# HGRN heads in pairs, emitted behind the RWKV stage

## The chip, the cores and the metric

The kernel is one program on one core of a Trainium2 chip. The metric is the device time of one execution in microseconds. Engines are named as in the profile: PE (TensorE), PEld (its weight loads), DVE (VectorE), ACT (ScalarE), POOL (GpSimd), SP (SyncE, which issues nearly all transfers).

## The reference

One layer for 512 tokens of width 1024, in float32: a norm, one wide projection, three mixers side by side (HGRN2, RWKV7, latent attention), a gated sum of their outputs, an output projection, a second norm and a gated feed-forward.

```python
h = rms_norm(x, mix_pre_g[l])
z = h @ w_cols
zq, zf, zi, zog, zrw, zcq, zckv, zkr, zgate, zvres = jnp.split(z, IN_SPLITS, axis=-1)
o_hg = hgrn2_mixer(zq, zf, zi, zog, lower_bounds[l], hgrn_onorm_g[l])
o_rw, v_first = rwkv7_mixer(zrw, ...)
o_mla = mla_mixer(zcq, zckv, zkr, cos, sin, ...)
merged = (g_hg * (o_hg @ w_branch[l, 0]) + g_rw * (o_rw @ w_branch[l, 1])
          + g_mla * (o_mla @ w_branch[l, 2]))
x = x + rms_norm(merged @ w_out[l], mix_post_g[l])
```

The change lies in the HGRN mixer. For each of eight heads of width 128 it runs a gated linear recurrence over the tokens:

```python
f = lower_bound + (1.0 - lower_bound) * jax.nn.sigmoid(zf32)
k = (1.0 - lower_bound) * jax.nn.sigmoid(-zf32)
...
o = jnp.einsum('bhts,bhsv->bhtv', scores, v) + jnp.einsum('bhtd,bhdv->bhtv', q * jnp.exp(b), state)
state = jnp.exp(b_last[:, :, 0, :, None]) * state + jnp.einsum('bhsd,bhsv->bhdv', kc * jnp.exp(b_last - b), v)
```

The result of each head is normalised and multiplied with `silu(zog)`.

## The kernel before

All activations stand feature by token, 128 features on the partitions and 512 tokens along the row. Large products are made three times over with operands split into a high and a low part (`mm3`, L137 to L139); a pair of 128-wide output columns runs through `stream`, which loads slabs of two 128-row blocks of weights, splits them on ACT (L205) and DVE (L132) and issues 12 matmuls of 128x512 for each slab into two `mmD` banks. These **dense matmuls** come from, in program order: `dense_z` (the projection, written to DRAM as `z`), `dense_gate` (the three gates, as `gth`), `branch(0)` on HGRN's output `ohg`, `branch(1)` on RWKV's output `orw`, and later `branch(2)` on the attention's output, `project` and `ffn`.

Beside them run three mixers, whose steps are small and depend on one another:

- RWKV (`rwkv`): for four groups of four heads a preparation (`rwkv_prep`, tiles `pr`), an inverse, a merge and a chain over eight chunks of 64 tokens (`rwkv_chain`, tiles `zus` and `yb`), with a normalisation at the end of a group.
- HGRN (`hgrn_head`, tiles `ph` in PSUM and names that begin with `h`): one head after another. It loads `f`, `q`, `v` and the output gate from `z`; makes `f` and `k`; takes a diagonal gram, then goes through the levels m = 1, 2, 4 ... 64. At each level it takes a gram of `k` and `q` (16 matmuls of 32x32 for levels 1 to 16, copied under a mask into `sd` by DVE, L804; 8 and 4 matmuls for levels 32 and 64, copied by ACT, L812), then multiplies one half of `q` (L817) and one half of `k` (L818) by the running gate `F`. Then come three transposes of `k`, the states (L834 to L838), the output `po` (L841, L843), squares and sums on ACT (L848), the power on POOL (L279), a scaling on ACT (L851), transposes, and the product with the gate (L855), which goes to `ohg`.
- The latent attention, MLA (`mla_low`, `mla_qv`, and eight times `mla_head`, tiles `pm`, `pmt`, `pmo`).

What sets the order: the code is written stage by stage, but each stage sits in a **lane**, a range of priorities (`lane`), and a scheduler merges the lanes at build time by its own estimate of when things are ready. HGRN's loads and first steps are in lane 6, its chain in lane 2, RWKV in lanes 5, 3 and 1, dense matmuls in lanes 7 and 0, MLA in lane 4. The merged order is then fixed for each engine: PE, DVE, ACT, POOL and SP each take their instructions in that order.

What can overlap is also set by memory. A pool that is opened gets free memory, or memory of pools that were closed ahead of it in program order, and then it waits for their last users. PSUM has eight banks: two `mmD` banks (`pD`), one each for `pC` and `pY` (RWKV's chain), two for `pR` (RWKV's preparation), two for `pH` (HGRN). `hgrn_open` is called ahead of `rwkv`, so HGRN has its own two banks and its own memory from the start, and its heads can run beside RWKV. MLA needs four banks and takes those of `pH` and `pR` when both are closed (`e4`, `e3` in `run`). All HGRN tiles but `hsg` are single, so a head's `k` or `q` is overwritten only when the head before it is through with it.

## Time and profile before

| what | value |
|---|---|
| median of 3 runs | 1433.51 us (1432.66 to 1435.68) |
| the profiled execution, its time and its span | 1434.43 us, 1432.6 us |
| instructions | 27571 |
| HGRN's tile `ph` on PE, first gram to last | 119.0 to 636.6 us |
| outputs of heads stored to `ohg`, first and last issue | 193.3 to 665.9 us |
| projection (`dense_z`), last copy | 568.4 us |
| gates (`dense_gate`), first and last | 583.7 to 813.0 us |
| RWKV's chain, last chunk's first product | 823.9 us |
| MLA's product with the values, first and last | 776.0 to 972.3 us |

How to read the profile's rows: a row of groups gives line, engine, operation, tile written and tiles read, shape, count, then busy time in us and the mean of one in ns, then the idle time of the engine just before such instructions and what ended it. A matmul of float32 operands is recorded twice, so a gram of 16 matmuls shows as x32. Matmuls overlap at their ends, so a matmul's duration is longer than the step from one to the next.

### The profile page before, as it was taken

How to read it: one execution, taken by the hardware profiler on the slowest of the kernel's cores; microseconds unless marked ns; L12 is line 12 of the kernel's file. 1: busy time of each engine (PE TensorE's matmuls, PEld its weight loads, DVE VectorE, ACT ScalarE, POOL GpSimd, SP SyncE). 2: the span in 40 equal slices, each digit the busy share in tenths (PEclk: the TensorE clock that was granted, in tenths of full speed). 3: DMA queues.
4: the chain of work that ended last, by engine and by line, in shares of the span. 5: the costliest groups of instructions: out<-in, count | busy, mean ns of one | idle time of the engine just before them, and what ended most of it. 6: DMA issues, size and time to landing. Idle time of an engine off the chain costs nothing.

```text
span 1432.6 us, 27571 instructions
## 1 busy us (share of the span) xinstructions
PE 1394.2 (97%) x9672; PEld 1113.5 (78%) x9672; DVE 877.6 (61%) x1918; ACT 639.3 (45%) x1283; POOL 155.8 (11%) x1028
## 2 busy tenths in 40 slices
PE   7999989999999999999999999999999999999997
PEld 6777767777777776777877788887788888888886
DVE  5667977868688587774745657665475444443234
ACT  5563555553736346434543445443354333332222
POOL 2110111121212021111201010001010000000000
PEclk9999999999999999999999999999999999999999
DMA  6555462444543535345523445445544333334223
GB/s 189 153 170 155 125 186 84 146 141 121 168 140 113 153 116 168 94 139 171 166 75 102 135 160 194 152 124 178 197 148 133 96 98 99 98 96 155 96 96 110
DMA packets 172602, 194.93 MB, mean 136 GB/s; under 512 B 33072, under 2 KB 125744, under 8 KB 172464
## 3 DMA queue, kind: packets, MB, share of 16 engines
q1 hardware_dynamic: 171072, 190.02, 43.8%
q10 hardware_dynamic: 1392, 3.15, 0.7%
q8 instruction: 77, 1.26, 0.4%
q14 instruction: 61, 0.50, 0.1%
HBM read 151.30 MB, written 41.81 MB: 135 GB/s over the span
## 4 chain that ended last, share of the span: by engine, by line
PE 84%; DMA 7%; ACT 3%; DVE 2%; issue 2%; SPq 1%; POOL 0%; DVEq 0%; POOLq 0%; ACTq 0%
PE mmD L137 18%; PE mmD L139 18%; PE mmD L138 17%; PE po L137 4%; PE po L139 4%; PE po L138 4%; PE pr L194 2%; DMA zr<-z 1%; PE pmo L1090 1%; PE yb L704 1%; PE pm L139 1%; PE pm L137 1%; PE pm L138 1%; DMA z<-zst 1%; DMA hz<-z 1%
## 5 line engine op out<-in xcount | busy, mean ns | idle before, releaser
L137 PE MATMUL mmD<-xH,whD 128*128 128x512 f32 (+1 forms) x1232 | 486.5, 396 | 10.0 <-ACT whD L205 4.8
L138 PE MATMUL mmD<-xL,whD 128*128 128x512 f32 (+1 forms) x1232 | 474.4, 386 | 0.0
L139 PE MATMUL mmD<-xH,wlD 128*128 128x512 f32 (+1 forms) x1232 | 456.7, 389 | 2.0 <-DVE wlD L132 1.9
L132 DVE TENSOR_TENSOR wlD<-wsD,whD 128x512 fp32r<-128x512 f32 x384 | 263.6, 687 | 307.7 <-ACT whD L205 293.5
L205 ACT CAST whD<-wsD 128x512 fp32r<-128x512 f32 x384 | 237.6, 619 | 417.6 <-PE mmD L138 258.7
L137 PEld LDWEIGHTS mmD<-xH,whD 128*128 128x128 f32 x1232 | 232.1, 189 | 60.0 <-issue 6.2
L139 PEld LDWEIGHTS mmD<-xH,wlD 128*128 128x128 f32 x1232 | 230.8, 189 | 51.6 <-DVE wlD L132 4.6
L138 PEld LDWEIGHTS mmD<-xL,whD 128*128 128x128 f32 x1232 | 232.8, 189 | 41.0 <-issue 0.4
L149 POOL MEMSET token<- 1x1 f32 x912 | 82.4, 90 | 763.4 <-PE mmD L139 746.2
L139 PE MATMUL po<-whD,fL 128*128 128x512 f32 x176 | 68.3, 390 | 0.0
L138 PE MATMUL po<-wlD,fH 128*128 128x512 f32 x176 | 68.3, 390 | 0.0
L137 PE MATMUL po<-whD,fH 128*128 128x512 f32 x176 | 50.9, 391 | 0.2
L279 POOL TENSOR_TENSOR rrs<-rtm,mhalf 128x1 f32<-128x1 f32 x8 | 4.7, 591 | 405.4 <-DVE rtm L274 368.3
L237 ACT COPY zst<-mmD 128x512 f32<-128x512 f32 x64 | 37.3, 583 | 23.1 <-PE mmD L139 22.6
L628 DVE TENSOR_TENSOR invtmp<-inv 64x30 f32<-64x30 f32 (+14 forms) x120 | 38.5, 321 | 10.6 <-DMA inv<-Ld 8.5
L629 DVE TENSOR_TENSOR inv<-inv,invtmp 64x30 f32<-64x30 f32 (+14 forms) x120 | 38.6, 322 | 2.3
L137 PEld LDWEIGHTS po<-whD,fH 128*128 128x128 f32 x176 | 32.9, 188 | 8.0 <-DVE y L1185 0.6
L139 PEld LDWEIGHTS po<-whD,fL 128*128 128x128 f32 x176 | 33.0, 188 | 7.1
L138 PEld LDWEIGHTS po<-wlD,fH 128*128 128x128 f32 x176 | 33.0, 188 | 7.0
L702 DVE SCALAR_TENSOR_TENSOR PV<-zus,gC,St 64x64 f32<-64x64 f32 x96 | 27.1, 282 | 15.8 <-PE zus L696 13.7
L682 POOL TENSOR_TENSOR St<-PV,gC 64x128 f32<-64x128 f32 x48 | 23.4, 486 | 41.8 <-DVE PV L702 30.9
L793 PEld LDWEIGHTS ph<-hq,hk 128*32 128x32 f32 x1536 | 17.9, 111 | 12.7 <-issue 4.0
(343 smaller groups left out, 2023.7 us busy)
## 6 DMA issues: line engine op xcount, KB each, us to landing
wsD<-in_w_in_dram SPq DMA_DIRECT2D x176, 256.0 KB, 3.0
wsD<-in_w_ffn_in_dram SPq DMA_DIRECT2D x96, 256.0 KB, 2.8
z<-zst SPq DMA_DIRECT2D x63, 256.0 KB, 2.8
wsD<-in_w_branch_dram SPq DMA_DIRECT2D x48, 256.0 KB, 2.7
wsD<-in_w_ffn_out_dram SPq DMA_DIRECT2D x44, 256.0 KB, 2.6
zr<-z SPq DMA_DIRECT2D x26, 256.0 KB, 3.0
gth<-zst SPq DMA_DIRECT2D x24, 256.0 KB, 2.2
th<-gth SPq DMA_DIRECT2D x24, 256.0 KB, 3.4
```

What stands on the lines that cost most here:

```text
L132: (eng or self.nc.vector).tensor_tensor(dst, src, high.bitcast(F32), op=ALU.subtract)
L137: first = mm(ps, lhsT=lh, rhs=rh, start=start, stop=False)
L138: mm(ps, lhsT=lh, rhs=rl, start=False, stop=False)
L139: return first, mm(ps, lhsT=ll, rhs=rh, start=False, stop=stop)
L149: token = self.nc.gpsimd.memset(self.token, 0.0).ins
L194: last = c()
L205: nc.scalar.copy(h, st)
L237: self.nc.scalar.copy(st[:m], ps)
L628: V.tensor_tensor(tv, cv, rv, op=ALU.mult)
L629: V.tensor_tensor(U[:, :j, j + 1:], U[:, :j, j + 1:], tv, op=ALU.add)
L682: nc.gpsimd.tensor_tensor(St[H[e]], PV[e][H[e], :, c, :], gC[H[e], :, c + 1:c + 2].to_broadcast([64, 2, C]), op=ALU.mult)
L702: V.scalar_tensor_tensor(nxt, zus[H[e], 2, q, :], gc, St[H[e], q, :], op0=ALU.mult, op1=ALU.add)
```

## The change

Two heads go through each step together, as one tile that is twice as wide: `hgrn_head(h)` becomes `hgrn_heads(h0)`, called four times. Element-wise steps are done once for both heads, except where a per-feature constant differs (L766 and L768, now once for each head); the masked copies, the multiplies of a level and the running gate have twice the width. Matmuls and transposes are as many as before, and those with 512 output columns keep a bank for each head. `pH` has four banks in place of two. And `hgrn_open` is called behind `rwkv()` and behind the closing of `e3`, so HGRN's banks and memory are those that RWKV's preparation (`pR`, `rt`) has left. Transfers are as many and as large as before.

```diff
-        self.pH = es.enter_context(tc.tile_pool(name="pH", bufs=2, space=PSUM))
-        self.hsc = self.t(self.hg, [P, NT, P], "hsc")
+        self.pH = es.enter_context(tc.tile_pool(name="pH", bufs=4, space=PSUM))
+        self.hsc = self.t(self.hg, [P, HH, NT, P], "hsc")
...
-        f = self.h_load(1, h, "hf")
-        k = self.t(hg, [P, S], "hk")
+        f = self.h_load(1, h0, "hf")
+        k = self.t(hg, [P, HH, S], "hk")
         A.activation(k, f, AF.Sigmoid, scale=-1.0)
         A.activation(f, f, AF.Sigmoid)
-        V.tensor_scalar(f, f, oml, lb, op0=ALU.mult, op1=ALU.add)
+        for j in range(HH):
+            lb, oml = self.lb[:, h0 + j:h0 + j + 1], self.oml[:, h0 + j:h0 + j + 1]
+            V.tensor_scalar(f[:, j], f[:, j], oml, lb, op0=ALU.mult, op1=ALU.add)
+            V.tensor_scalar(k[:, j], k[:, j], oml, None, op0=ALU.mult)
...
+        q, k, f = flat(q), flat(k), flat(f)
+        N = HH * S
         def gram():
-            g = self.t(pH, [P, NT, HB], "ph")
-            for o in range(0, S, HB):
+            g = self.t(pH, [P, W, HB], "ph")
+            for o in range(0, N, HB):
...
-                g = self.t(pH, [P, NT, m], "ph")
-                for i in range(NT):
+                g = self.t(pH, [P, W, m], "ph")
+                for i in range(W):
...
+        for j, po in enumerate(pos):
+            for i in range(NT):
+                A.activation(on[:, j, i, :], po[:, i, :], AF.Copy, scale=rs[:, j * NT + i:j * NT + i + 1])
...
         self.rwkv_open(e1, e2, e3)
+        self.rwkv()
+        e3.close()
         self.hgrn_open(e4)
-        self.rwkv()
-        for h in range(8):
-            self.hgrn_head(h)
+        for h in range(0, 8, HH):
+            self.hgrn_heads(h)
         e4.close()
-        e3.close()
```

The order on PE before, at the diagonal gram of the last head (`ph` written from `hq` and `hk`; `zus` is RWKV's chain, `mmD` a dense matmul):

```order
L793 MATMUL ph_9326<-hq_9309,hk_9303 32x32 x6
L691 MATMUL zus_7191<-zsb_7198,LM_5909 64x64 x4
L793 MATMUL ph_9326<-hq_9309,hk_9303 32x32 x10
L137 MATMUL mmD_3676<-xH_7_108,whD_3679 128x512
L138 MATMUL mmD_3676<-xL_15_116,whD_3679 128x512
L139 MATMUL mmD_3676<-xH_7_108,wlD_3680 128x512
L137 MATMUL mmD_3676<-xH_8_109,whD_3679 128x512
```

Fifteen dense matmuls and eight of RWKV's follow before this head's next gram. The order on PE now, at the third pair, from the end of the second one's output to the third one's last level (`yb` is written here from `y`, in RWKV's last normalisation):

```order
L873 MATMUL ph_8476<-cst,hkT_8434 128x128 x3
L782 MATMUL ph_8507<-cst,hz_8497 128x128 x4
L803 MATMUL ph_8520<-hq_8494,hk_8486 32x32 x32
L803 MATMUL ph_8555<-hq_8494,hk_8486 32x32 x32
L803 MATMUL ph_8593<-hq_8494,hk_8486 32x32 x32
L726 MATMUL yb_7681<-cst,y_7420 128x128 x4
L803 MATMUL ph_8631<-hq_8494,hk_8486 32x32 x32
L726 MATMUL yb_7696<-cst,y_7420 128x128 x4
L803 MATMUL ph_8669<-hq_8494,hk_8486 32x32 x32
L803 MATMUL ph_8707<-hq_8494,hk_8486 32x32 x32
L820 MATMUL ph_8745<-hq_8494,hk_8486 32x32 x16
L820 MATMUL ph_8768<-hq_8494,hk_8486 64x64 x8
```

Between the steps stands no dense matmul any more. The first pair's first step on PE comes behind the last matmul of RWKV's preparation and behind RWKV's last merge; the last dense matmul of the gates comes ahead of the second pair's gram of level 16; and the next dense matmul, the first of branch 0, behind the fourth pair's last transpose.

A second place, MLA's last heads. On PE before (`pm` scores, `pmt` transposes, `pmo` products with the values), around a block's transpose in the seventh head:

```order
L1074 MATMUL pm_11721<-krL_10572,qr_10606 128x384
L1086 MATMUL pmt_11694<-cst,mp_11690 128x128
L1070 MATMUL pm_11745<-uh_2071_11674,uh_2065_11657 128x512
L1071 MATMUL pm_11745<-ul_2072_11675,uh_2065_11657 128x512
L1072 MATMUL pm_11745<-uh_2071_11674,ul_2066_11658 128x512
L1073 MATMUL pm_11745<-krH_10571,qr_10606 128x512
L1074 MATMUL pm_11745<-krL_10572,qr_10606 128x512
L139 MATMUL mmD_10230<-xH_1654_9980,wlD_10301 128x512
L137 MATMUL mmD_10230<-xH_1655_9981,whD_10300 128x512
```

Ten dense matmuls (the fence shows the first two) stand there before the block's product `pmo`. On PE now, the same place in the seventh head:

```order
L1092 MATMUL pm_11461<-krL_10288,qr_10322 128x512
L139 MATMUL mmD_11633<-oL_1720_10562,whD_11681 128x512
L140 MATMUL mmD_11633<-oH_1712_10554,wlD_11682 128x512
L139 MATMUL mmD_11634<-oL_1720_10562,whD_11681 128x512
L140 MATMUL mmD_11634<-oH_1712_10554,wlD_11682 128x512
L1108 MATMUL pmo_11394<-mpT_11412,mv_10455 128x128
L1104 MATMUL pmt_11430<-cst,mp_11426 128x128 x2
L138 MATMUL pm_11495<-cqH_10196,whU_1983_11491 128x512
```

Only four stand there, and two more in the rest of that head; they belong to branch 2 (`oH`, `oL`), since those of branches 0 and 1 are used up. From one head's first score to the next one's, the dense matmuls were 40, 46, 148, 54, 56, 55 and 48, and are 60, 54, 57, 18, 6, 6 and 6. From the output projection on, the order is that of before.

## Prediction

> **What bounds the kernel now.** I read the page first, then the stages by window, then single groups by shape.

> ```profile
> PE 1394.2 (97%) x9672; PEld 1113.5 (78%) x9672; DVE 877.6 (61%) x1918; ACT 639.3 (45%) x1283; POOL 155.8 (11%) x1028
> PE 84%; DMA 7%; ACT 3%; DVE 2%; issue 2%; SPq 1%; POOL 0%; DVEq 0%; POOLq 0%; ACTq 0%
> 120.00:660.00 540.00, 526.93 (x5206) 401.65 (x5205) 408.34 (x1003) 270.68 (x580) 88.33 (x539) 0.99 0.46 135
> 660.00:980.00 320.00, 319.27 (x1860) 260.52 (x1859) 195.81 (x459) 150.97 (x310) 36.09 (x275) 1.00 0.47 144
> 1160.00:1200.00 40.00, 40.00 (x178) 33.12 (x177) 17.93 (x27) 13.64 (x23) 0.00 (x0) 1.00 0.34 98
> L793 PE MATMUL ph<-hq,hk x1536: 196/196/218, 119.0 to 636.6; 128*32 128x32 f32 x192
> 110.00:670.00 560.00, 73.00 (x1976) 56.81 (x1976) 27.68 (x80) 33.95 (x136) 0.99 0.47 137
> ```

> TensorE is the bound: 97% busy, 84% of the chain that ended last. In the windows (after the length: PE, PEld, DVE, ACT, POOL busy, clock, DMA share, GB/s) it idles 13.1 us of 540 while HGRN runs and 0.7 us of the 320 of MLA. So a change pays only if PE does less, or idles less; there is 13 us of idleness to win in HGRN's stretch, and none after it. A dense matmul takes 40.00/178 = 0.225 us.

> The HGRN grams run from 119.0 to 636.6 us, eight heads in some 550 us. The last window is that of the HGRN tile `ph` alone: 73.0 us of PE. A head is a long chain of short steps over PE, DVE, ACT and POOL, and it costs nothing now because dense matmuls (`mmD`) stand between its steps. The kernel is fast because the chains have **cover**; the question for the change is who covers them in the new order.

> **The change part by part.** *The arithmetic* stays: as many matmuls of the same sizes, so PE's own work is unchanged. *The order* is what moves. PE takes its instructions in program order; the rows shown with the change say that up to the end of RWKV's preparation no HGRN step is left on PE, that pairs 1 and 2 stand among dense matmuls, and that behind the last gate matmul, before the first matmul of branch 0, stand the end of pair 2 (from its gram of level 16), all of pair 3 and all of pair 4, with no dense matmul among them. What is queued behind them is MLA's first matmul and branch 0, which itself needs all of `ohg`.

> So I price **a pair that runs alone**, from these rows (durations of one head's steps):

> ```profile
> L798 DVE TENSOR_TENSOR hq<-hq,hf 128x512 f32<-128x512 f32 x8 | 5.6, 701 | 0.0
> L817 DVE TENSOR_TENSOR hq<-hq,hF 128x256 f32<-128x256 f32 x48 | 20.2, 421 | 4.2 <-PE ph L810 4.1
> L804 DVE COPY_PREDICATED hsd<-hgm,ph 128x128 f32<-128x128 uint8 x40 | 11.8, 294 | 5.1 <-PE ph L793 4.9
> L838 DVE SCALAR_TENSOR_TENSOR hst<-hst,hF,ph 128x128 f32<-128x128 f32 x16 | 5.4, 340 | 0.1
> L855 DVE SCALAR_TENSOR_TENSOR hsg<-ph,hon,hsg 128x512 f32<-128x512 f32 x8 | 6.0, 744 | 1.1 <-PE ph L854 0.9
> L831 ACT COPY hkT<-ph 128x384 f32<-128x384 f32 x8 | 3.8, 480 | 6.9 <-PE ph L829 6.8
> L848 ACT ACTIVATE hkT<-ph 128x128 f32<-128x128 f32 x32 | 8.4, 277 | 6.1 <-PE ph L843 6.0
> L848 ACT ACTIVATION_READ_ACCUMULATOR hkT<-ph 128x1 f32 x32 | 6.6, 207 | 0.0
> L851 ACT ACTIVATE hkT<-ph,hrs 128x128 f32<-128x128 f32 x32 | 9.3, 372 | 6.8 <-POOL token L149 6.8
> L279 POOL TENSOR_TENSOR rs<-ss,mhalf 128x8 f32<-128x8 f32 x8 | 13.2, 1652 | 19.9 <-DVE ss L538 18.7 <-PE mmD L138 1.2
> 615.71 0.46 PE L793 MATMUL ph<-hq,hk 128*32 128x32 f32 x32
> 616.10 0.50 PE L137 MATMUL mmD<-xH,whD 128*128 128x512 f32 x1
> ```

> - DVE: a level's two multiplies become 512 wide, 0.70 us as in L798; 7 levels x 2 = 9.8. The full product of `q` and `f` is 1024 wide: 0.70 + 2 x (0.70 - 0.42) = 1.26. Five masked copies, 256 wide, about 0.43 each (0.29 and half of what 256 more elements cost): 2.2. Diagonal 0.4, states 2 x (0.28 + 2 x 0.34) = 1.9, last output 0.74. Together 16.3 us.
> - PE: a head's gram of 16 matmuls (32 records) is 0.46 us long and lets the next start after 0.39, so a pair's is 0.85; six are 5.1, the two block levels about 1.0, and transposes, `dS`, `po` about 2.4 as far as nobody overlaps them. 8.5 us.
> - ACT: two `hkT` copies 0.96, eight squares 8 x (0.277 + 0.207) = 3.9, eight scalings 3.0. 7.8 us.
> - POOL: the power on 128x8, 1.65 us.

> Each waits for the one before: a level's multiplies need the last gram read, the next gram needs both products. In series 34.3 us; the second head's states and squares lie partly beside the first head's, hand-overs add; I take **33 us**. Bounds: 27 (DVE plus its waits for grams, the tail halved) and 43 (two heads in sequence, 20 us each by the same rows at half width, and some waits).

> The uncovered stretch is then: rest of pair 2, from its last gram, 19 (two levels more, then the tail); pairs 3 and 4, 66; RWKV's last three chunks and its normalisation, in line with them on DVE and PE, 4; hand-over to MLA, 9:

> ```profile
> 668.36 4.38 DMA mz<-z
> 676.40 0.79 PE pm L953 x8
> ```

> MLA's pools take HGRN's memory and its four PSUM banks, so its first load starts when HGRN has ended, and its first matmul came 8 us after the load's start; before, dense matmuls covered that. In sum **98 us**. In it lies PE work that was paid before too: 56% of the grams and 102 larger steps, about 4.6 heads of 73.0/8 = 9.1 us, x 0.39/0.46 since records overlap: 36, and RWKV's rest, 5. Loss: 98 - 41 = **57 us**.

> **The clock** is the second term. The one place where PE had much the same sparse work is 208 to 214:

> ```profile
> 208.00:210.00 2.00, 0.88 (x5) 0.32 (x3) 1.22 (x3) 0.00 (x0) 0.18 (x2) 1.00 0.58 146
> 210.00:212.00 2.00, 0.75 (x50) 0.64 (x52) 1.94 (x7) 0.90 (x2) 0.00 (x0) 1.00 0.87 268
> 212.00:214.00 2.00, 1.48 (x59) 1.35 (x52) 1.97 (x3) 2.00 (x5) 0.00 (x0) 0.67 0.77 251
> 214.00:216.00 2.00, 2.00 (x9) 1.90 (x9) 2.00 (x6) 1.97 (x3) 0.00 (x0) 0.50 0.57 214
> 218.00:220.00 2.00, 2.00 (x7) 1.61 (x6) 0.00 (x1) 1.32 (x3) 0.09 (x1) 0.62 0.11 37
> 210.98 0.46 PE L793 MATMUL ph<-hq,hk 128*32 128x32 f32 x32 [1.20 <-DVE hk L818]
> 213.49 1.87 PE L535 MATMUL pr<-cst,t 128*128 128x2 f32 x8 [0.52 <-ACT t L531]
> 100.41 1.05 PE pr L535 x8
> ```

> After 4 us at 40% busy the granted clock fell to 0.50, and eight small matmuls took 1.87 us instead of 1.05. A lone pair keeps PE busy a quarter to a third of the time, so I expect half clock through most of the stretch: 2.4 pairs x 8.5 us of PE on the path x 0.78 = **16 us**, between 0 and 20. [...]

> **MLA** is the third. 384 dense matmuls of branches 0 and 1 are left to cover eight heads; the order spends most of them early: from the fourth head on it leaves 18, and then 6 to each of the last four, where a head has 57 now:

> ```profile
> 888.67:911.51 22.84, 14.18 (x57) 10.37 (x56) 1.36 (x2) 0.00 (x0) 1.00 0.51 163
> 888.67:911.51 22.84, 22.84 (x124) 19.54 (x123) 14.20 (x34) 9.93 (x22) 1.76 (x19) 1.00 0.51 163
> ```

> (the first row is `mmD` alone, the second all). A head's own PE work is 22.84 - 57 x 0.225 = 10.0, with 6 dense ones 11.4; its own DVE and ACT work some 9 and 7. The floor is 11.4, full series 27; two score banks let blocks overlap, so near the floor: 14. The fourth head, 10.0 + 18 x 0.225 = 14, loses nothing then; four heads x 2.6 = 10, and the last head's transposes and copies, which have nothing behind them, 3: **13 us** (0 to 4 x 15.6 + 3 = 65).

> **What may come back**: with HGRN gone, some of the 13.1 us of idleness before 660 us, and switches between dense and small work; I take 4 (0 to 15). PE, not DVE's instruction count, was the bound there, so the halved count of DVE and ACT steps is worth nothing by itself. More SP and ACT work is not issued: loads stay 128x512 each, two per name.

> Sum: 57 + 16 + 13 - 4 = 82 us, on the profiled execution's 1434.4 (its span of 1432.6 and 1.8 around it; the median of the runs is 0.9 lower): **1517 us**.

> **The rivals.**
> - *The clock stays full* in the stretch: the sum without that term, 1501. [...] Against: the fall at 213 us.
> - *The pair does not do what it says*: its two heads run after one another, since a step twice as wide costs DVE nearly twice as much (421 against 701 ns). 40 us for 33, x 2.6: 1535; with MLA heads at 20 us, five x 6 more, 1565. For it: the single banks of transposes and outputs in MLA. Against: the fixed part of each step, about 140 ns, is saved.
> - *A short stretch*: engines overlap better, 27 us a pair, full clock, MLA at its floor: 57 - 2.6 x 6 = 41, less 4: 1470.
> - *Faster*: HGRN's departure gives back all 13.1 us of idleness up to 660 us, and the 2 us that dense matmuls lost at half clock at 215: 1419. It decides if the stretch loses under 15 us, so if it lasts 56 and a pair some 16 us: DVE's own 16.3, with PE, ACT and POOL wholly beside it. The chain's waits speak against it.

> **How the numbers follow.** Forecast 50%, full clock 22%, pair in sequence or slow MLA 17%, short stretch 6%, faster 3%, no change 2%. The range takes in the bounds of chain, clock and MLA as far as they are not all at one end: 1470 to 1585. Faster by over 0.2% (about what a measurement can tell from no change) 0.03, within 0.02, slower 0.95.

> **What would show it.** Right: past 650 us a stretch of some 100 us or more in which PE is mostly idle, released by DVE and ACT, tile names `ph`, clock near 0.5; MLA heads at 13 to 15 us with PE idle a few us each; everything from the output projection on as before. Wrong: PE over 80% busy there (then the chain is shorter than the rows say), clock 1.00 (first rival), or MLA heads at 20 us. The forecast fails as a whole if dense matmuls are not exhausted where the order says.

## The result, and the profile after

| | kernel before | kernel after |
|---|---|---|
| median of the runs | 1434.6 us (1432.66 to 1438.4, 4 runs) | 1506.96 us (1503.12 to 1509.23, 4 runs) |
| profiled execution: span, mean granted clock | 1432.6 us, 0.996 | 1501.3 us, 0.967 |

The change makes the kernel slower: ratio 1.0498, with a 95% interval of 1.0465 to 1.0531. The forecast was 1517 us. The profiled execution took 1503.12 us, the shortest of the four.

The page after (busy time and share by engine, two rows of the span in 40 slices, the chain by engine):

```profile
PE 1411.8 (94%) x9672; PEld 1130.6 (75%) x9672; DVE 873.1 (58%) x1794; ACT 622.6 (41%) x1231; POOL 154.0 (10%) x1024
PE   7999999999999999999555999998999999999998
PEclk9999999999999999999665899999999999999999
PE 80%; DMA 5%; DVE 5%; issue 5%; ACT 3%; POOL 1%; SPq 1%; DVEq 0%; POOLq 0%; ACTq 0%
```

PE has as many instructions as before and is busy 17.6 us longer (1411.8 against 1394.2): the same work in longer records. Most of it is the lower clock: in the stretch below PE is busy 38.8 us at a clock of 0.50, where a pair's gram takes 1.08 us, against 0.76 at full clock, which makes some 11 us (an estimate from these three numbers). It also idles 51.1 us longer (89.5 against 38.4); the two make up the 68.7 us by which the span grew. Three slices of the page, from 713 to 826 us, hold nearly all of it: PE half busy and the clock at 0.5 to 0.6.

The windows (length, then PE, PEld, DVE, ACT, POOL busy, clock, DMA share, GB/s): up to the last dense matmul of the gates; from there to MLA's first dense cover; MLA's last heads; and two short ones inside the stretch.

```profile
120.00:697.50 577.50, 572.55 (x4647) 433.60 (x4647) 394.38 (x859) 255.40 (x484) 96.67 (x646) 1.00 0.48 143
697.50:823.20 125.70, 68.31 (x1310) 58.49 (x1308) 67.71 (x150) 45.50 (x132) 10.11 (x11) 0.67 0.23 75
985.00:1042.50 57.50, 53.69 (x324) 46.31 (x323) 37.70 (x111) 30.65 (x76) 0.80 (x9) 1.00 0.09 28
740.00:760.00 20.00, 10.79 (x201) 9.94 (x202) 10.46 (x22) 7.06 (x14) 0.00 (x0) 0.50 0.22 66
780.00:800.00 20.00, 10.36 (x258) 9.43 (x259) 9.36 (x18) 3.87 (x9) 0.00 (x0) 0.50 0.01 2
```

Ahead of the stretch PE idles 4.95 us in 577.5, where the kernel before idled 13.1 in 540. In the stretch it idles 57.4. DVE, ACT and POOL are not full there either: each waits for another. The edges of the stretch are these two matmuls (PE's instructions in order of time):

```profile
697.68 0.39 PE L140 MATMUL mmD<-xH,wlD 128*128 128x512 f32 x1
...
819.36 3.54 PE L971 MATMUL pm<-ones,msq 128*128 128x1 f32 x16 [9.53 <-DMA mkv<-z]
```

From the end of the first to the start of the second pass 121.3 us. Where the time of a lone pair goes is seen on DVE in order of time: the diagonal grams (L807) of pairs 3 and 4, two levels of pair 4, and its end.

```profile
725.56 0.42 DVE L807 TENSOR_TENSOR hsd<-ph,cst 128x256 f32<-128x256 f32 x1
...
771.11 0.42 DVE L807 TENSOR_TENSOR hsd<-ph,cst 128x256 f32<-128x256 f32 x1 [0.80 <-PE ph L803]
...
775.38 1.22 DVE L788 SCALAR_TENSOR_TENSOR hsg<-hsg,hz 128x1024 f32<-128x1024 f32 x1 [2.72 <-ACT hsg L787]
...
779.43 0.44 DVE L814 COPY_PREDICATED hsd<-hgm,ph 128x256 f32<-128x256 uint8 x1 [1.29 <-PE ph L803]
779.77 0.68 DVE L827 TENSOR_TENSOR hq<-hq,hF 128x512 f32<-128x512 f32 x1
780.37 0.68 DVE L828 TENSOR_TENSOR hk<-hk,hF 128x512 f32<-128x512 f32 x1
782.34 0.44 DVE L814 COPY_PREDICATED hsd<-hgm,ph 128x256 f32<-128x256 uint8 x1 [1.29 <-PE ph L803]
...
808.84 0.75 DVE L874 SCALAR_TENSOR_TENSOR hsg<-ph,hon,hsg 128x512 f32<-128x512 f32 x1 [3.46 <-PE ph L873]
809.87 0.75 DVE L874 SCALAR_TENSOR_TENSOR hsg<-ph,hon,hsg 128x512 f32<-128x512 f32 x1 [0.28 <-PE ph L873]
```

A level takes 2.91 us, of which DVE works 1.6 and waits 1.29 for the next gram at a clock of 0.50. From one pair's diagonal gram to the next one's it is 45.6 us, and from the last one's to its last output 39.5 (770.31 and 810.62 are the ends of the third and the fourth pair).

Behind the stretch little is lost. MLA's last five heads (the last 100 of its 160 products) go through the window 985 to 1042.5 at 11.5 us each, with PE idle 0.8 us a head. MLA's last product was at 972.3 us before and is at 1042.6 now (matmuls that write `pmo`, of before and of after):

```profile
L1090 PE MATMUL pmo<-mpT,mv x160: 270/275/377, 776.0 to 972.3; 128*128 128x128 f32 x160
```

```profile
L1108 PE MATMUL pmo<-mpT,mv x160: 270/275/377, 921.5 to 1042.6; 128*128 128x128 f32 x160
```

That is 70.3 us later; the rest of the span is 460.3 us before and 458.7 after. So the whole loss stands ahead of MLA's end.

### The profile page after: what moved, and what is told of

The parts are those of the page before. It is cut to its first block, busy times and chain, and to the rows that moved or that the text cites. A ratio compares the mean times of both kernels' runs of the same rounds, so it can differ in the third digit from the quotient of the medians.

```text
span 1501.3 us, 27415 instructions
## 1 busy us (share of the span) xinstructions
PE 1411.8 (94%) x9672; PEld 1130.6 (75%) x9672; DVE 873.1 (58%) x1794; ACT 622.6 (41%) x1231; POOL 154.0 (10%) x1024
## 3 DMA queue, kind: packets, MB, share of 16 engines
q8 instruction: 77, 1.26, 0.4%
## 4 chain that ended last, share of the span: by engine, by line
PE 80%; DMA 5%; DVE 5%; issue 5%; ACT 3%; POOL 1%; SPq 1%; DVEq 0%; POOLq 0%; ACTq 0%
PE mmD L138 18%; PE mmD L140 17%; PE mmD L139 17%; PE po L138 4%; PE po L140 3%; PE po L139 3%; PE pr L195 2%; PE yb L705 1%; DMA zr<-z 1%; PE pm L138 1%; PE pm L139 1%; PE pm L140 1%; DMA z<-zst 1%; PE pmo L1108 1%; PE yb L690 1%
## 5 line engine op out<-in xcount | busy, mean ns | idle before, releaser
L138 PE MATMUL mmD<-xH,whD 128*128 128x512 f32 (+1 forms) x1232 | 488.8, 398 | 3.7 <-DVE rs L1206 1.2
L140 PE MATMUL mmD<-xH,wlD 128*128 128x512 f32 (+1 forms) x1232 | 449.9, 387 | 1.6 <-DVE wlD L133 1.5
L138 PEld LDWEIGHTS mmD<-xH,whD 128*128 128x128 f32 x1232 | 231.7, 189 | 56.5 <-POOL token L150 4.7
L140 PEld LDWEIGHTS mmD<-xH,wlD 128*128 128x128 f32 x1232 | 230.8, 188 | 51.1 <-DVE wlD L133 4.0
L139 PEld LDWEIGHTS mmD<-xL,whD 128*128 128x128 f32 x1232 | 232.6, 189 | 40.3 <-DVE xL L133 0.2
L140 PE MATMUL po<-whD,fL 128*128 128x512 f32 x176 | 68.3, 390 | 0.0
L139 PE MATMUL po<-wlD,fH 128*128 128x512 f32 x176 | 68.3, 390 | 0.0
L138 PE MATMUL po<-whD,fH 128*128 128x512 f32 x176 | 50.9, 391 | 0.2
L629 DVE TENSOR_TENSOR invtmp<-inv 64x30 f32<-64x30 f32 (+14 forms) x120 | 38.8, 323 | 13.4 <-DMA inv<-Ld 10.8
L803 PE MATMUL ph<-hq,hk 128*32 128x32 f32 x1536 | 23.3, 215 | 23.7 <-DVE hk L828 18.7
L630 DVE TENSOR_TENSOR inv<-inv,invtmp 64x30 f32<-64x30 f32 (+14 forms) x120 | 38.8, 323 | 2.7
L138 PEld LDWEIGHTS po<-whD,fH 128*128 128x128 f32 x176 | 32.9, 188 | 8.0 <-DVE y L1203 0.6
```

What stands on the lines that cost most here:

```text
L138: first = mm(ps, lhsT=lh, rhs=rh, start=start, stop=False)
L139: mm(ps, lhsT=lh, rhs=rl, start=False, stop=False)
L140: return first, mm(ps, lhsT=ll, rhs=rh, start=False, stop=stop)
L629: V.tensor_tensor(tv, cv, rv, op=ALU.mult)
L630: V.tensor_tensor(U[:, :j, j + 1:], U[:, :j, j + 1:], tv, op=ALU.add)
L803: mm(g[b:b + HB, o // P, :], lhsT=k[:, t], rhs=q[:, t], start=True, stop=True)
```

## The experiments

Each was run beside the kernel before on the same chip, and ratios are to that. The changed kernel was not run again with them: differences to it are to its 1506.96 us.

### The place alone: single heads behind RWKV

The changed kernel with `hgrn_head`, `h_load` and `hsc` of the kernel before; `pH` keeps four banks.

```diff
-    def hgrn_heads(self, h0):
+    def hgrn_head(self, h):
...
         self.rwkv()
         e3.close()
         self.hgrn_open(e4)
-        for h in range(0, 8, HH):
-            self.hgrn_heads(h)
+        for h in range(8):
+            self.hgrn_head(h)
```

> Heads one by one as before, but their pool opened behind the RWKV stage, with four banks, as in the change. The order on PE leaves about five and a half heads behind the last gate matmul without a dense matmul. Cover theory (the loss comes from the place, not from the width): a lone head takes about 24 us by the rows, so the uncovered stretch grows from 125 to some 150 us and the time is about 1530 us (1515 to 1545), slower than the change. Rival (the wide steps cost the time): the time returns towards that of before, 1460 us or less.

Measured: 1559.62 us, ratio 1.0862 (1.0826 to 1.0898), above the range that was expected. The rival falls: the place alone costs 123 us, and the width, which was thought to be what costs, gives 53 us back. Lone heads follow one another on DVE like this (diagonal grams of the last three heads, and two levels of the last one):

```profile
796.78 0.29 DVE L797 TENSOR_TENSOR hsd<-ph,cst 128x128 f32<-128x128 f32 x1 [3.74 <-PE ph L793]
...
822.68 0.29 DVE L797 TENSOR_TENSOR hsd<-ph,cst 128x128 f32<-128x128 f32 x1 [3.09 <-PE ph L793]
...
848.12 0.29 DVE L797 TENSOR_TENSOR hsd<-ph,cst 128x128 f32<-128x128 f32 x1 [3.51 <-PE ph L793]
...
856.44 0.30 DVE L804 COPY_PREDICATED hsd<-hgm,ph 128x128 f32<-128x128 uint8 x1 [0.86 <-PE ph L793]
...
858.26 0.30 DVE L804 COPY_PREDICATED hsd<-hgm,ph 128x128 f32<-128x128 uint8 x1 [0.86 <-PE ph L793]
```

A lone head takes 26 us, two 52, and a lone pair 40 to 46; a level of one head takes 1.82 us and of a pair 2.91. A head's ends and waits weigh more than the prediction's bound for two heads in sequence, 20 us each, allowed.

Pairs at the old place, beside RWKV, were not run (their pool holds 44 KB for each partition, the sum of its tiles, and would lie beside RWKV's pools), so what they would be worth there stays open.

### More dense work behind the gates

Behind `dense_gate`, eight groups of 24 dense matmuls of the same shape, paced as they are; nothing reads their result.

```diff
+    def idle_work(self, groups):
+        for g in range(groups):
+            p = self.t(self.pD, [P, S], "mmD")
+            for k in range(KD):
+                xh = self.h[0][k]
+                group = self.mm3(p, xh[:, :P], xh[:, P:2 * P], xh, xh, k == 0, k == KD - 1)
...
             self.dense_gate(n)
+        self.idle_work(8)
```

> The change, with 192 more dense matmuls behind the gates whose result nobody reads (43 us of PE work at 0.225 us each). Cover and clock theory: they fill the idle time at the third pair, the granted clock stays at 1.00 there, a level's step falls from 2.9 us to about 2.3, and the time is within 10 us of the change's 1507 although PE has 43 us more to do; the fourth pair stays bare, with the clock near 0.5. Rival (PE work adds up, the clock does nothing): about 1550 us.

Measured: 1530.49 us, ratio 1.0656 (1.0623 to 1.0688): neither. 43 us of work cost 23.5. The windows show it lying beside the ends of pairs 2 and 3, where PE is now full at full clock, while pair 4 is as bare as before:

```profile
720.00:740.00 20.00, 20.00 (x144) 15.72 (x142) 8.47 (x27) 6.83 (x28) 3.36 (x18) 1.00 0.09 28
740.00:760.00 20.00, 20.00 (x280) 16.01 (x279) 12.49 (x18) 5.25 (x8) 4.71 (x22) 1.00 0.37 114
800.00:820.00 20.00, 7.34 (x304) 6.66 (x304) 10.72 (x19) 3.23 (x8) 0.00 (x0) 0.51 0.01 2
```

About half of the work fell into holes; the rest, since PE is full there, stood ahead of the pairs' steps in PE's queue. From diagonal gram to last output, pair 2 took 68.7 us in place of 53.0, pair 3 49.5 in place of 44.8, and pair 4 40.3 in place of 39.5. So this work, though it filled holes, made the chains longer by about half of itself; what matters is where it stands, as the runs on the clock below show.

### The same cover, later

Ten of the twelve gate streams are held until the first pair has begun.

```diff
+        for n in gates[:-HELD]:
+            self.dense_gate(n)
...
         for h in range(0, 8, HH):
             self.hgrn_heads(h)
+            if h == 0:
+                self.hold = self.mark
+                self.lane(7)
+                for n in gates[-HELD:]:
+                    self.dense_gate(n)
+                self.hold = None
```

> The change, with the last ten of twelve gate streams made to wait for the first step of the first pair, so that RWKV's stage cannot use them up. By the order, pairs 1 to 3 then have dense matmuls between their steps, the fourth has none, and a piece of RWKV's chain of some 25 us has few. Cover theory: 1470 us (1455 to 1485). Rival (the wide chain or the banks cost the time wherever it stands): no change, 1507 us.

Measured: 1518.03 us, ratio 1.0569 (1.0537 to 1.0601): 11 us slower than the change, where 37 faster were expected. The expectation failed. Two windows of it, the end of RWKV's preparation and pair 4:

```profile
560.00:580.00 20.00, 1.92 (x46) 1.63 (x48) 10.96 (x33) 0.00 (x0) 0.96 (x1) 0.50 0.22 46
...
780.00:800.00 20.00, 8.32 (x336) 7.34 (x336) 9.90 (x16) 4.41 (x11) 0.00 (x0) 0.68 0.16 54
```

RWKV's preparation, with its inverse and last merge, now stands bare, and though nothing dense is in its way, pair 1's diagonal gram comes only 10 us earlier (592.4 against 602.6). The hole moved; it did not close. That suggested another reading: not the supply of cover but the length of two chains, one behind the other, sets the time. The next two runs test it.

### No cover at all, in both orders

All twelve gate streams (130 us of PE) are held until the last HGRN output is made, once in the changed kernel and once in the kernel before.

```diff
-        for n in (*range(8, 16, 2), *range(0, 8, 2), *range(16, 24, 2)):
-            self.dense_gate(n)
...
             self.hgrn_heads(h)
+        self.hold = self.mark
+        self.lane(7)
+        for n in (*range(8, 16, 2), *range(0, 8, 2), *range(16, 24, 2)):
+            self.dense_gate(n)
+        self.hold = None
```

> The changed kernel with all 12 gate streams (576 dense matmuls, 130 us of PE) held until the last pair's last output. Theory: RWKV's preparation and then the four pairs are two chains in line, and their length, not the dense work, sets the time; the gates only lay beside them. RWKV's preparation should then end at some 590 us as before, bare from about 500 on, the pairs take 45 us each with little beside them, to about 770, and the gates follow at full speed to 900, with the hand-over to MLA hidden: 1575 us, 1555 to 1590. Rival: the chains are shorter when nothing dense stands between their steps (preparation over by 560, pairs 33 us each, 690), so the gates end about where MLA starts now: 1500 to 1510.

> The kernel before, with the same 12 gate streams held until the last single head's last output. Theory: there the heads run beside RWKV's preparation, so both chains are over by some 620 us, and the gates then lie beside RWKV's chunks and MLA, which have their own work: only 500 to 620 is thinner on PE, 15 to 40 us lost, 1450 to 1475 against 1436. Rival: what counts is only how much dense work is left as cover, not which chains run side by side; then this kernel loses as much against the one before as the changed kernel with its gates last loses against the changed one, 70 us: 1505.

Measured: the changed kernel with its gates last 1581.0 us (ratio 1.1015, 1.0983 to 1.1047), the kernel before with its gates last 1464.83 (1.021, 1.0175 to 1.0245). Both are where the theory put them, and both rivals fall (the second kernel is 2.1% slower, 1.75 to 2.45). The HGRN grams of the first and of the second (matmuls on `ph`: shortest, median and longest in ns, then the first and the last start):

```profile
L807 PE MATMUL ph<-hq,hk x1536: 189/241/263, 582.4 to 753.7; 128*32 128x32 f32 x192
```

```profile
L797 PE MATMUL ph<-hq,hk x1536: 189/196/262, 119.7 to 608.3; 128*32 128x32 f32 x192
```

With no gate beside it, RWKV's part ahead of the first pair (preparation, inverse and merge of its last group) still ends only at 582 us, 18 us earlier than in the change, and the four pairs then take until 776 us, 48 us a pair. The granted clock is 0.54 there from 500 to 582 us; how much of that length is the clock's was not measured. What the first pair waits for is the last group's inverse, a chain of 60 steps on DVE (from 537.8 to 564.7 us; 546.9 to 581.2 in the change), and its transfer out and back. PE has nothing to do meanwhile, for 22.10 us:

```profile
572.69 0.28 PE L193 MATMUL yb<-lsq,LM 32*32 32x32 f32 x2 [22.10 <-DVE lsq L653]
```

RWKV's last merge in the kernel before, in the change and here (the second time is the start of the last matmul):

```profile
L194 PE MATMUL yb<-LM,lsq x248: 191/191/212, 221.0 to 656.3; 32*32 32x32 f32 x124
```

```profile
L195 PE MATMUL yb<-LM,lsq x248: 191/191/212, 198.4 to 598.8; 32*32 32x32 f32 x124
```

```profile
L196 PE MATMUL yb<-LM,lsq x248: 191/191/257, 198.7 to 581.0; 32*32 32x32 f32 x124
```

So RWKV's part does end earlier in the change, where HGRN is not beside it, by 57 us, but the pairs that follow it need 211 us there. Behind the pairs of this run, 130 us of gates that earlier lay beside the chains are still to be done. In the old order the last of eight single heads takes its last gram at 608 us, because the heads ran beside RWKV's preparation all the time from 119.7 us on. So taking the gates away from the chains costs 30 us in the old order and 74 in the new.

### Two banks, and a second load buffer

Two edits of single sizes in the changed kernel: `pH` back to two banks; two buffers for `lnx`, whose loads DVE waits for in RWKV's last normalisation.

```diff
-        self.pH = es.enter_context(tc.tile_pool(name="pH", bufs=4, space=PSUM))
+        self.pH = es.enter_context(tc.tile_pool(name="pH", bufs=2, space=PSUM))
```

```diff
-                x = self.t(rt, [P, S], "lnx")
+                x = self.t(rt, [P, S], "lnx", bufs=2)
```

> The changed kernel with two PSUM banks for ph instead of four. Theory: in the bare stretch a pair is one serial chain of gram, masked copy, multiplies, so two banks carry it; only the tail (two po kept until they are scaled, and transposes of the next pair's hz done ahead) has to wait. 1509 to 1514 against 1507 of the change. Rival: the four banks are what lets one pair's beginning overlap the end of the one before; then each of the three hand-overs between pairs loses 4 to 5 us, 1520 to 1525.

> The change, with two buffers in place of one for the loads of RWKV's normalisation (lnx), whose waits stand in DVE's order between the levels of the third pair. If these loads lengthen the third pair by the waits that the trace shows (1.2 to 1.8 us each, four times), the time falls by 4 to 7 us, and the waits of L738 for DMA go under 2 us in sum. Rival (HGRN's own chain ends last there anyway): within 2 us of 1507.

Measured: 1522.55 us with two banks (ratio 1.0607, 1.0577 to 1.0637), so the banks are worth 15 us and the theory falls. The time is where the rival put it, the place only in part. From diagonal gram to diagonal gram or last output, pairs 3 and 4 take 44.7 and 40.3 us, against 45.6 and 39.5 in the change. On DVE, pair 1's last output and pair 2's diagonal gram:

```profile
679.75 0.73 DVE L874 SCALAR_TENSOR_TENSOR hsg<-ph,hon,hsg 128x512 f32<-128x512 f32 x1
687.75 0.42 DVE L807 TENSOR_TENSOR hsd<-ph,cst 128x256 f32<-128x256 f32 x1 [0.40 <-PE ph L803]
```

8.0 us lie between their starts, 3.6 in the change; the next two hand-overs lose 3.0 and 1.2 us. That makes 8.7 of the 20 us by which the last output comes later. Pair 1's own gram was 8.5 us late, 3.8 of them already in RWKV's last merge (602.6 against 598.8 us); why was not found. The gates end no later (696.9 us), so more of pair 2 is left for the bare stretch.

With two `lnx` buffers: 1508.87 us, ratio 1.0507 (1.0479 to 1.0536), no change, as the rival had it. The three waits for loads in pair 3, of 1.18, 1.76 and 1.18 us, become two, of 0.48 and 1.49, and from its diagonal gram to the next one's it still is 45.3 us; those waits were not on the path.

### The clock

Unread dense matmuls behind the grams of pairs 3 and 4, where PE waits for DVE. In a first form there were also groups of 2 and of 8 in the pairs' ends; in the second only those behind grams, 64 in all.

```diff
+    def warm(self, after, n=4):
+        if self.warming:
+            p, xh = self.t(self.pD, [P, S], "mmD"), self.h[0][0]
+            for i in range(n):
+                mm = self.nc.tensor.matmul(p, lhsT=xh[:, :P], rhs=xh, start=i == 0, stop=i == n - 1)
...
         def gram():
...
+            self.warm(last)
             return g
```

> The changed kernel, with unread dense matmuls behind each gram (4), transposition and dS (2) and po (8) of pairs 3 and 4: 56 a pair, 25 us of PE in all, put where PE waits for DVE and ACT anyway. Theory: the half clock lengthens the grams on the path, and the extra work keeps the clock at 0.9 to 1.0; a level's wait for its gram falls from 1.29 to about 0.85 us and the stretch by 13 to 17 us: 1490 to 1496. Rival 1: the clock falls all the same or the grams' length is hidden: 1504 to 1510. Rival 2: the extra matmuls stand in front of the next gram, as the 43 us of filler did, and cost half their own length: 1519.

> As the run with unread matmuls behind every step, but only behind the eight grams and blocks of pairs 3 and 4 (4 each, 64 in all); nothing extra in their ends, where the groups of 8 stood in front of the second head's products. Theory: the half clock costs 0.43 us a level on the path (a level took 2.48 us at clock 0.9 to 1.0 there, 2.91 in the changed kernel), two times eight levels, less what waits for RWKV's normalisation in pair 3: 4 to 7 us less than the changed kernel, 1500 to 1503. Rival: DVE's other waits in the level section take the gain up, 1505 to 1509.

Measured: the first form 1505.57 us, ratio 1.0495 (1.0459 to 1.0531), no different from the change, where 1490 to 1496 had been expected; the second 1497.16, ratio 1.0421 (1.0403 to 1.0439), 10 us better, more than was expected. Two neighbouring levels of pair 4 in the second form:

```profile
780.36 0.45 DVE L824 COPY_PREDICATED hsd<-hgm,ph 128x256 f32<-128x256 uint8 x1 [1.20 <-PE ph L812]
...
782.85 0.45 DVE L824 COPY_PREDICATED hsd<-hgm,ph 128x256 f32<-128x256 uint8 x1 [0.86 <-PE ph L812]
```

At a clock of 1.00 in that window (0.50 in the change) the wait for a gram is 0.86 us in place of 1.29, and a level takes 2.49 in place of 2.91. From pair 3's diagonal gram to pair 4's last output the change takes 85.1 us, the second form 76.2, the first 82.9: there the levels were as quick, but a group of 8 stood ahead of the second head's products (2.1 us) and groups of 2 among the steps before them.

### The gate's product, later

```diff
-        A.activation(sg, zg, AF.Tanh, scale=0.5)
-        V.scalar_tensor_tensor(sg, sg, 1.0, zg, op0=ALU.add, op1=ALU.mult)
...
+        A.activation(sg, zg, AF.Tanh, scale=0.5)
+        gate = V.scalar_tensor_tensor(sg, sg, 1.0, zg, op0=ALU.add, op1=ALU.mult)
...
         for b in range(0, P, HB):
             A.copy(sc[b:b + HB, :, b:b + HB], sd[b:b + HB])
```

> The changed kernel with the product of tanh and gate (hsg, 128x1024, 1.23 us on DVE) put behind a pair's last level instead of ahead of its first masked copy, where DVE waited 1.28 and 2.72 us for ACT's tanh in pairs 3 and 4. Theory: this wait is part of why a pair takes 40 us and not 33; it and the product leave the path in two bare pairs, and the product then lies in a wait of the pair's end: 2 times 1.2 plus 2.7 plus at most 1.3, so 4 to 6 us less than the changed kernel, 1501 to 1503. Rival: ACT's tanh then stands ahead of the copies of the end, which lose what the start wins: 1505 to 1509.

> Both edits, the warm levels and the late gate. If both costs are real and lie one behind the other, the sum: 8 to 13 us less than the changed kernel, 1494 to 1499. If they are the same wait told twice, no better than the better of the two alone.

Measured: alone 1503.0 us, ratio 1.0454 (1.043 to 1.0479); with the warm levels 1497.94, ratio 1.0428 (1.041 to 1.0447). The interval of the first overlaps that of the change, so its total settles nothing; in the trace the same two pairs take 80.7 us in place of 85.1, what the theory asked for, but pair 3 begins 2.7 us later, so the last output comes only 1.7 us earlier. With both edits the two pairs take 76.2, like the warm levels alone: the savings do not add, and which of DVE's waits takes the second one up stays open.

## Why the prediction was right, and where its sizes were off

The direction, the mechanism and the place were right: behind the last gate matmul a stretch in which PE is half idle (68.3 us busy of 125.7), released by DVE and ACT, at a granted clock of 0.67 (0.50 in the two short windows), and then a kernel as before. 1507 lies 10 us below the forecast (whose terms add up to 1516.4), and nearer to the rival with a full clock, 1501; the time does not decide between the two, the clock in the rows does. By the prediction's own terms:

| term | predicted | measured |
|---|---|---|
| uncovered stretch, clock included | 98 + 16 = 114 us | 121.3 us |
| a pair alone | 33 us, plus its share of the clock (some 7) | 45.6 and 39.5 us |
| PE idle in the stretch | 98 - 41 = 57 us | 57.4 us |
| clock | 16 us | PE busy 17.6 us longer; 10 us on the path shown |
| MLA's last heads | 13 us (14 us a head) | some 4 us (11.5 us a head) |
| comes back ahead of the stretch | 4 us | 8 us |

- **The uncovered stretch.** 7 us longer than foretold. Pair 4 came out at what the sum gives with the clock in it, 33 + 8.5 x 0.78 = 39.6 us, though it holds a wait that the sum left out (2.72 us for the gate's tanh at the head of DVE's queue) and the product of 1.22 us behind it, so other steps were reckoned a little long. Pair 3 is 6 us longer: RWKV's last normalisation, put at 4 us in all, stands between its levels on DVE. The equality of 57 with 57.4 us of idleness is partly luck, since the 98 us were reckoned at full clock.
- **The clock.** It fell, as the rows of 208 to 214 us had suggested; the rival at 1501 with a full clock is excluded by the rows at 0.50. That it costs time on the path was only argued then; the warm levels show it, with 10 us got back, 9 of them in pairs 3 and 4.
- **MLA.** The mis-sized term. Single banks and six dense matmuls a head were expected to leave PE idle 2.6 us a head; it idles 0.8: heads overlap more than the floor plus a margin allowed. 13 us should have been 4.
- **What comes back** was 8 us instead of 4: once HGRN has gone, PE idles 4.95 us up to the gates' end in place of 13.1.
- Together 75 us (57.4 idle in the stretch and 17.6 of longer records), plus 4, less 8, are 71 us, where the two profiled spans differ by 68.7.
- **The rival of two heads in sequence** is excluded: 52 us for two lone heads against 40 to 46 for a pair. The width does what it says, and pays 53 us at this place.

What the prediction did not have is the sharper reason that the two runs without gates gave. It spoke of cover that runs out. But more cover (23.5 us slower) and later cover (11 us slower) did not help. The kernel before let two long chains, RWKV's preparation and HGRN's heads, run beside each other: RWKV's last merge came at 656 us and HGRN's last output at 666. The change set them in line. RWKV's part became 57 us shorter by that (599 us), but the four pairs behind it take 211 us, so HGRN ends at 811, 145 us later than before. With no gates beside them the two chains in line still end only at 776: of 130 us of dense work some 35 show, and the length of the two chains does the rest.

## What to carry to other kernels

When a change moves a chain of short dependent steps, ask first which other chain it ran beside, and how much shorter that one gets without it (57 us here, against 211 us of pairs that then stand behind it). More or later cover did not make up for that here, and what stood ahead of a chain's next step in PE's queue made it longer. Making the steps of a chain wider paid where the chain stood alone (53 us). And where the dense work ran out here, the granted clock fell to 0.50, so the steps that are left should be priced at the clock that rows of work as sparse as that show (a level of a pair took 2.91 us at 0.50 and 2.49 at 1.00).

## What the runs showed of the hardware that was not expected

The granted clock fell at points that the holes ahead of them do not explain. PE's rows after (in brackets the hole ahead of an instruction), at the stretch's start and in pair 4:

```profile
702.48 0.70 PE L820 MATMUL ph<-hq,hk 128*32 128x32 f32 x32 [1.16 <-DVE hk L828]
...
718.08 0.45 PE L692 MATMUL zus<-zsb,LM 64*64 64x64 f32 x8 [0.30 <-DVE zsb L688]
718.91 0.98 PE L705 MATMUL yb<-PV,LM 64*64 64x64 f32 x8 [0.39 <-DVE PV L693]
...
770.30 0.76 PE L803 MATMUL ph<-hq,hk 128*32 128x32 f32 x64
...
778.29 1.08 PE L803 MATMUL ph<-hq,hk 128*32 128x32 f32 x64 [4.73 <-DVE hk L828]
781.20 1.08 PE L803 MATMUL ph<-hq,hk 128*32 128x32 f32 x64 [1.83 <-DVE hk L828]
```

At 718.08 us eight matmuls of 64x64 take 0.45 us, and at 718.91 eight of the same size take 0.98; the longest hole since the last dense matmul is the 1.16 us at 702. In pair 4 the gram at 770.30 ran at full clock and the one at 778.29 at half; the hole of 4.73 us lies between them. But the clock fell at 773.66 us, only 0.1 us into that hole (from 773.60 to 773.80 it is 0.65 on average, before it 1.00, behind it 0.50), and then stayed at 0.50 up to 801 us with holes of 1.83 us and PE busy about half of the time (10.36 of the 20 us from 780 on).

```profile
701.98:705.40 3.42, 1.90 (x54) 1.72 (x55) 2.14 (x5) 1.79 (x5) 0.00 (x0) 1.00 0.04 10
715.64:719.05 3.41, 2.64 (x38) 1.91 (x34) 2.15 (x10) 2.21 (x17) 0.81 (x1) 1.00 0.41 122
719.05:722.46 3.41, 2.68 (x16) 2.09 (x16) 2.10 (x3) 2.55 (x10) 0.83 (x1) 0.50 0.10 37
763.42:766.84 3.42, 0.32 (x2) 0.21 (x2) 0.26 (x2) 1.40 (x9) 1.64 (x1) 1.00 0.52 153
766.84:770.25 3.41, 3.41 (x16) 2.88 (x15) 1.44 (x2) 2.02 (x7) 0.00 (x0) 0.50 0.20 77
770.25:773.66 3.41, 1.57 (x129) 1.32 (x128) 1.61 (x3) 0.59 (x1) 0.00 (x0) 1.00 0.65 226
773.66:777.08 3.42, 0.00 (x0) 0.00 (x0) 1.70 (x3) 1.06 (x1) 0.00 (x0) 0.50 0.04 9
```

Behind the step in which PE was busy throughout (766.84) the clock came back; it fell behind steps with 0.32, 1.57 and 2.64 us of work, and did not behind one with 1.90 (701.98). So PE's busy time in one step does not by itself give the clock of the next, and what does was not found.

In the second form of the warm levels the clock was down too behind a hole of 3.12 us (up to the gram at 776.39), and it came back while four spare matmuls with a gram on both sides of them kept PE busy, 2.61 and 2.44 of 3 us in the first two of these windows of that run (clock 0.52, 0.91 and then 1.00):

```profile
776.00:779.00 3.00, 2.61 (x68) 2.14 (x68) 1.71 (x4) 0.00 (x0) 0.00 (x0) 0.52 0.02 5
779.00:782.00 3.00, 2.44 (x70) 1.45 (x68) 1.78 (x4) 0.00 (x0) 0.00 (x0) 0.91 0.03 5
782.00:785.00 3.00, 2.36 (x98) 1.80 (x100) 1.62 (x3) 1.61 (x4) 0.00 (x0) 1.00 0.00 0
```

So here the stage whose PE had more to do, some 0.9 us of unread work in every level (four matmuls at 0.225 us, an estimate), was through sooner (pairs 3 and 4 in 76.2 us in place of 85.1).
